# A four-layer encoder trunk on one core: loading and splitting its first input in quarters

## The chip, the cores and the metric

The kernel runs on one core of a Trainium2 chip. The core has TensorE (matrix products and transpositions), VectorE, ScalarE, GpSimd and SyncE (which here issues most DMAs). The metric is the device time of one execution in microseconds (us).

## The reference

Input x is 256 tokens by 1024 columns, float32. Six stages follow each other; each ends in a layer norm of a scaled x plus the stage's result:

```python
def swiglu(x, w_in, w_out):
    gu = x @ w_in
    g, u = gu[..., :D_FF], gu[..., D_FF:]
    return (jax.nn.silu(g) * u) @ w_out

for l in range(2):
    x = layer_norm(ALPHA * x + 0.5 * swiglu(x, ffn_w_in[l, 0], ffn_w_out[l, 0]), ...)
    y = mlstm_mixer(x, ...) if l % 2 == 0 else window_attention(x, ...)
    x = layer_norm(ALPHA * x + y, ...)
    x = layer_norm(ALPHA * x + 0.5 * swiglu(x, ffn_w_in[l, 1], ffn_w_out[l, 1]), ...)
```

`ffn_w_in[l, i]` is 1024 by 5632, `ffn_w_out[l, i]` 2816 by 1024. This document is on the first microseconds of the first `swiglu`.

## The kernel before

**Split numbers.** Every float32 operand of a product is split into a rounded high part and a low part (what is left), and a product is three: high with high, high with low, low with high. ScalarE makes the high part by a cast (`w_hi`, `xT_hi`), VectorE the low part by a subtraction (`w_lo`, `xT_lo`), in each case for weights and for x turned (`xT`).

**Words of weights.** Weights come in words of 128 partitions by 1024 columns (512 KB). A word of `w_in` for the first stage is two blocks of 128 rows by 512 columns, so a word takes 2 blocks x 2 token tiles x 3 = 12 products of 128x512. Class `Weights` loads words from SyncE's queue (`W.load`) into `w_raw` (four buffers), and splits them (`high` and `low`; ten buffers each of `w_hi` and `w_lo`). A buffer of `w_raw` is free for its next word when `low` is done with it. The first word is split in two halves of 512 columns, which ScalarE and VectorE handle one after the other; the load itself is one DMA.

**Turned x.** The products want x with columns on partitions. `to_xT(t, src, bank, halves)` turns token tile t (128 tokens): per half (512 columns) four transpositions on TensorE into one PSUM bank `py`, then `split_evac`, which writes `xT_hi` (ScalarE, or VectorE when `high` is given) and `xT_lo` (VectorE).

**The start.** `load_x(t, h)` loads x in four DMAs of 256 KB (two tiles, two halves), all from ScalarE's queue. `warm(n)` turns the identity n times on TensorE; nothing reads the result. The first stage then runs, in the order of the code: 14 idle turns, the first half of tile 0 turned (VectorE makes both parts), word 0 split, 8 idle turns, and for each of the eight words (m is 0 for g and 1 for u, a is 0 to 3) its 12 products. For words 0 and 1 of m = 0 the order of products is written out in `first_mm`: `mm(t, i, j)` is tile t with x's part i (0 high, 1 low) and the word's part j. Tile 1's first half is turned after the first two products, and both second halves between word 0 and word 1. From word 2 on `b_mm` has no special order.

**What sets the order.** The schedule is the order in which the code emits instructions; each engine works its own list in order. `Paced` keeps a running model of the engines' and queues' times, with which `Weights.fill` decides between products what ScalarE and VectorE split next. So an edit of the start can change the order of later casts and subtractions.

**Waits.** A DMA tells of its landing by one of eight semaphores, which the DMAs of SyncE and ScalarE use in turn; the ninth waits for the landing of the first, and so on.

Of the kernel before, what the change touches and what calls it, by code (L numbers as in the profile page):

```python
# [16 lines left out]
D = 1024  # L17
# [18 lines left out]
FB = [1, 0, 1, 0, 2, 0, 0, 0, 1, 1, 2]  # L36
CT = [0, 1]
DC = 1
EX = [1, 2, 2, 2, 2, 2, 2, 2]
RS = [0, 0, 1, 0, 1, 0, 0, 0, 0, 0, 0, 3, 0, 0, 1, 0, 1, 0, 1, 0, 0, 0, 2, 0, 0, 0, 1, 0, 1, 2, 0, 0, 0, 1, 0, 0, 2, 0, 1, 1, 0, 0, 0, 0, 2, 2, 0, 1]  # L40
XP = [4, 0, 1, 2]
# [24 lines left out]
class Paced:  # L66
# [45 lines left out]
    def load(self, ap, source, engine=None):  # L112
        if engine is not None:
            engine.dma_start(ap, source)
        elif isinstance(source, list):
            for k, src in enumerate(source):
                self.nc.sync.dma_start(ap[:, k].rearrange("p (m f) -> p m f", m=src.shape[1]), src)
        else:
            self.nc.sync.dma_start(ap, source)
        self.moving(0, ap, LANDING, LOADING * int(np.prod(ap.shape[1:])) / 1024, ISSUING)  # L120
# [70 lines left out]
class Weights:  # L191
# [33 lines left out]
    def load(self, most=None):  # L225

        nc = self.nc
        n = 0
        once = False
        while most is None or n < most:  # L230
            next_ = []
            for tag, todo in self.todo.items():
                if not todo:
                    continue
                first = self.first[todo[0]]
                if tag != "w_raw":
                    if self.free[tag] and not once and first < self.used + self.span:
                        next_.append((first, tag, tag))
                elif self.free[tag]:
                    next_.append((first, tag, tag))  # L240
                elif todo[0] < self.send and self.free["v_raw"]:
                    next_.append((first, tag, "v_raw"))
            if not next_:
                break
            _, tag, in_ = min(next_)
            once = once or tag != "w_raw"
            i = self.todo[tag].pop(0)
            pool, bufs = {"w_raw": (self.pool, RAW_BUFS), "v_raw": (self.spool, V_RAW)}.get(in_, (self.rooms, S_RAW))
            t = pool.tile([128, D], F32, name=tag, tag=in_, bufs=bufs)
            nc.load(t.rearrange("p (k f) -> p k f", k=self.words[i]["k"]), self.words[i]["src"])  # L250
            self.raw[i], self.words[i]["in"] = t, in_
            self.free[in_] -= 1
            n += 1
# [72 lines left out]
    def low(self):  # L326

        nc = self.nc
        i, hi = self.half.pop(0)
        p = self.plan[i]  # L330
        k, scale, raw = p["k"], p["scale"], self.raw[p["word"]]
        lo = self.pool.tile([128, D], FR, name="w_lo", tag="w_lo", bufs=RING)
        if i == 0:
            for j in range(2):
                s_ = slice(j * 512, j * 512 + 512)
                nc.vector.tensor_sub(lo[:, s_], raw[:, s_], hi[:, s_].bitcast(F32))
        elif scale is None:
# [109 lines left out]
def trunk_kernel(ctx: ExitStack, tc: tile.TileContext, x, ffn_w_in, ffn_w_out, ln_g, ln_b, ml_w_in, ml_gate_b,  # L447
                 ml_norm_g, ml_w_out, at_w_in, at_sink, at_w_out, out):
    nc = Paced(tc.nc)
# [79 lines left out]
    for j, (kind, l, i, _) in enumerate(stages):  # L529
        if kind == "ffn":  # L530
# [13 lines left out]
            for g in range(SEVENS):  # L544
                c0 = 768 + 512 * g
# [25 lines left out]
    for p in reversed(plan):  # L571
        if p["needs"] is not None:
            q = plan[p["needs"]]
            q["due"] = min(q["due"], p["due"] - p["behind"])

    xt = [state.tile([128, D], F32, name=f"x{t}", tag=f"x{t}") for t in range(2)]

    def load_x(t, h):
        s_ = slice(h * 512, h * 512 + 512)
        nc.load(xt[t][:, s_], x[0, t * 128:(t + 1) * 128, s_], nc.nc.scalar)  # L580

    xT = (state.tile([128, 8, S], FR, name="xT_hi", tag="xT_hi"),
          state.tile([128, 8, S], FR, name="xT_lo", tag="xT_lo"))

    W = Weights(nc, wpool, rooms, words, plan, after)
    load_x(0, 0)
    W.load(1)
    load_x(1, 0)
    W.load(1)
    load_x(0, 1)  # L590
    load_x(1, 1)
    W.load()
    nc.scalar.preload_act_table(AF.Silu)

    ident = consts.tile([128, 128], F32, name="ident")
# [28 lines left out]
    def pair(p, *idx):  # L624
        return p[0][idx], p[1][idx]

    def wbank(shape=(128, 512)):
        return psum.tile(list(shape), F32, name="pw", tag="pw", bufs=4)

    def ybank(shape=(128, 512)):  # L630
        return psum.tile(list(shape), F32, name="py", tag="py", bufs=4)

    A = slice(None)

    def tok(t):
        return slice(t * 128, (t + 1) * 128)

    def split_evac(dst, src, scale=None, high=None, wait=False):
        if scale is None:
            (high or nc.scalar.copy)(dst[0], src)  # L640
            low = lambda: nc.vector.tensor_sub(dst[1], src, dst[0].bitcast(F32))
            if wait:
                W.when_ready(low, dst[0])
            else:
                low()
        else:
            nc.scalar.activation(dst[0], src, AF.Copy, scale=scale)
            nc.vector.scalar_tensor_tensor(dst[1], src, scale, dst[0].bitcast(F32), op0=OP.mult, op1=OP.subtract)

    turned = {}  # L650

    def to_xT(t, src, bank, halves=range(2), high=None):
        for h in halves:
            p = bank((128, 4, 128))
            for k in range(4):
                nc.tensor.transpose(p[:, k], src[:, (4 * h + k) * 128:(4 * h + k + 1) * 128], ident)
            split_evac(pair(xT, A, slice(4 * h, 4 * h + 4), tok(t)), p, high=high)
            turned[t, h] = p

    def warm(n):  # L660

        p = ybank((128, 4, 128))
        for j in range(n):
            nc.tensor.transpose(p[:, j % 4], ident, ident)
# [103 lines left out]
    def emit_x(t, last):  # L768
        if not last:
            to_xT(t, xt[t], ybank)  # L770

    def ffn(l, i, n, pending, last):
        with ExitStack() as ph:
# [9 lines left out]

            start = pending is None
            if start:
                warm(14)
                to_xT(0, xt[0], ybank, (0,), nc.vector.tensor_copy)
                W.split(1)
                warm(8)
            hs, pieces = [], []  # L790

            def tr(hB, t, h):
# [15 lines left out]

            def first_mm(ps, a):

                def mm(t, i, j):
                    for k in (2 * a, 2 * a + 1):
                        nc.tensor.matmul(ps[t], xT[i][:, k, tok(t)], pieces[a][j][:, k % 2], start=i == j == k == 0,
                                         stop=False)

                if a == 1:
                    for t in range(2):
                        to_xT(t, xt[t], ybank, (1,))
                pieces.extend(W.take(1))
                mm(0, 0, 0)  # L820
                if a == 0:
                    to_xT(1, xt[1], ybank, (0,))
                    W.split(2)
                mm(0, 1, 0)
                if a == 0:
                    mm(0, 0, 1)
                mm(1, 0, 0)
                if a == 0:
                    mm(1, 0, 1)
                mm(1, 1, 0)  # L830
                if a == 1:
                    mm(0, 0, 1)
                    mm(1, 0, 1)

# [39 lines left out]
            if start:  # L874
                sg = {}
                for m in range(2):
                    ps = [wbank(), wbank()]
# [132 lines left out]
            ps = [wbank(), wbank()]  # L1010
            pieces = []
# [325 lines left out]
    def attn(l, n, pending, last):  # L1337
        with ExitStack() as ph:
# [98 lines left out]
            def scores(j, between):  # L1437
# [54 lines left out]
            def turn(j, sb, p):  # L1492
# [140 lines left out]
```

## Time and profile before

| | us |
|---|---|
| median of 3 runs | 911.12 (910.35 to 911.18) |
| the profiled execution | 910.79 |
| its span, first to last instruction | 909.1 |
| TensorE busy | 900.3 |
| VectorE busy | 799.6 |
| ScalarE busy | 570.3 |

In the rows of the profile, PE is TensorE's products and transpositions (MATMUL in both cases), PEld its loads of the stationary operand (LDWEIGHTS), DVE is VectorE, ACT is ScalarE, POOL is GpSimd, SP is SyncE; a q behind an engine is its sequencer issuing DMAs. `py<-ident` is an idle turn, `py<-ident,x` a turn of x, `pw<-w_hi,xT_hi` a product. All engine instructions go through one helper, so they share one line (L182) and are told apart by their tiles. A row of the timeline is: start, length, engine, line, operation, tiles, shape, count, and in brackets the engine's idle time before it and what ended it; equal instructions that follow each other are merged. A row of groups ends in: busy us, mean ns of one, idle time before. A row of stretches gives busy us (and count) of PE, PEld, DVE, ACT and POOL, then granted clock, DMA share and GB/s. A DMA issue row ends in its size and the time from issue to landing; a queue row is packets, MB, share of the 16 engines' time.

### The profile page before, as it was taken

The page shows a single profiled execution, that of the slowest core. Times are in us where ns is not written, and L with a number is a line of the kernel's source. Part 1 is how long each engine was busy: PE and PEld are TensorE (multiplying, and loading weights), DVE is VectorE, ACT ScalarE, POOL GpSimd, SP SyncE. Part 2 cuts the span into 40 slices and gives each one's busy share as a digit, 9 for nine tenths or more (in the row PEclk, how much of TensorE's full clock was granted, in tenths as well). Part 3 has the DMA queues.
Part 4 walks back from the last instruction along what each step waited for, and adds up shares of the span by engine and source line. Part 5 has one row for each costly group of instructions (what it writes and reads, how often), then busy time and mean ns, then how long its engine had stood idle before and what let it go on. Part 6 is the DMA issues. An engine that isn't in the chain of part 4 may idle for free.

```text
span 909.1 us, 12461 instructions
## 1 busy us (share of the span) xinstructions
PE 900.3 (99%) x4427; PEld 749.5 (82%) x4427; DVE 799.6 (88%) x961; ACT 570.3 (63%) x785; POOL 152.1 (17%) x190
## 2 busy tenths in 40 slices
PE   9999999999999999999999999999999999999996
PEld 7888888889988888888888888888886788888885
DVE  6999999886799898999988899998868789899986
ACT  5776777356664666776636677765568556676760
POOL 0111123113211011211011112110325301111110
PEclk9999999999999999999999999999999999999999
DMA  8999998546637898998868889986444587899851
GB/s 290 367 330 249 287 276 217 164 138 183 212 106 247 297 237 235 292 278 242 236 197 279 254 248 280 281 220 216 140 140 140 170 294 219 202 296 281 251 140 47
DMA packets 100703, 208.53 MB, mean 229 GB/s; under 512 B 6904, under 2 KB 21264, under 8 KB 100640
## 3 DMA queue, kind: packets, MB, share of 16 engines
q1 hardware_dynamic: 82368, 173.04, 54.4%
q0 software_dynamic: 17696, 33.65, 22.2%
q10 hardware_dynamic: 576, 1.05, 0.3%
q8 instruction: 35, 0.57, 0.2%
q14 instruction: 28, 0.23, 0.1%
HBM read 206.65 MB, written 1.05 MB: 228 GB/s over the span
## 4 chain that ended last, share of the span: by engine, by line
PE 98%; DVE 1%; issue 0%; DVEq 0%; POOL 0%; POOLq 0%
PE pw L182 63%; PE py L182 35%; DVE w_lo L182 0%; DVE x L182 0%; DVE stats L182 0%; DVE e L182 0%; DVE s_raw L182 0%; DVEq L1629 0%; DVE mv L182 0%; POOL ji L597 0%; DVE ident L182 0%; DVE rs L182 0%; DVEq L182 0%; POOLq L597 0%; POOLq L1620 0%
## 5 line engine op out<-in xcount | busy, mean ns | idle before, releaser
L182 DVE TENSOR_TENSOR w_lo<-w_raw,w_hi 128x1024 fp32r<-128x1024 f32 (+1 forms) x213 | 255.8, 1222 | 25.4 <-ACT w_hi L182 23.5
L182 ACT CAST w_hi<-w_raw 128x1024 fp32r<-128x1024 f32 (+1 forms) x213 | 218.9, 1050 | 77.1 <-PE py L182 22.2
L182 DVE TENSOR_TENSOR w_lo<-s_raw,w_hi 128x1024 fp32r<-128x1024 f32 x192 | 228.7, 1220 | 18.8 <-ACT w_hi L182 18.7
L182 ACT CAST w_hi<-s_raw 128x1024 fp32r<-128x1024 f32 x192 | 196.6, 1054 | 58.8 <-PE py L182 25.0
L182 PE MATMUL pw<-w_hi,xT_hi 128*128 128x512 f32 x480 | 189.4, 396 | 0.0
L182 PE MATMUL pw<-w_hi,xT_lo 128*128 128x512 f32 x480 | 186.9, 391 | 0.0
L182 PE MATMUL pw<-w_lo,xT_hi 128*128 128x512 f32 x480 | 186.7, 390 | 0.1
L123 POOL DMA_DIRECT2D s_raw<-in_ffn_w_in_dram x64 | 77.4, 1211 | 484.0 <-DVE s_raw L182 222.3
L182 PE MATMUL py<-w_hi,h_hi 128*128 128x512 f32 x349 | 138.2, 396 | 0.0
L182 PE MATMUL py<-w_hi,h_lo 128*128 128x512 f32 x349 | 136.2, 390 | 0.0
L182 PE MATMUL py<-w_lo,h_hi 128*128 128x512 f32 x349 | 136.0, 390 | 0.0
L182 PEld LDWEIGHTS pw<-w_lo,xT_hi 128*128 128x128 f32 x480 | 90.3, 188 | 18.8 <-DVE w_lo L182 1.3
L182 PEld LDWEIGHTS pw<-w_hi,xT_lo 128*128 128x128 f32 x480 | 90.1, 188 | 19.1
L182 PEld LDWEIGHTS pw<-w_hi,xT_hi 128*128 128x128 f32 x480 | 90.1, 188 | 17.2
L182 PE MATMUL pw<-w_hi,S_lo 128*128 128x512 f32 x256 | 99.7, 389 | 0.0
L182 PE MATMUL pw<-w_lo,S_hi 128*128 128x512 f32 x256 | 99.7, 389 | 0.0
L182 PE MATMUL pw<-w_hi,S_hi 128*128 128x512 f32 x256 | 99.7, 389 | 0.0
L182 DVE TENSOR_TENSOR s_raw<-s_raw,s_raw 128x1024 f32<-128x1024 f32 x64 | 76.8, 1220 | 0.3
L182 PEld LDWEIGHTS py<-w_hi,h_lo 128*128 128x128 f32 x349 | 65.5, 188 | 14.0
L182 PEld LDWEIGHTS py<-w_lo,h_hi 128*128 128x128 f32 x349 | 65.7, 188 | 13.0
L182 PEld LDWEIGHTS py<-w_hi,h_hi 128*128 128x128 f32 x349 | 65.6, 188 | 12.8
L182 PEld LDWEIGHTS pw<-w_lo,S_hi 128*128 128x128 f32 x256 | 48.1, 188 | 10.0
(203 smaller groups left out, 1099.0 us busy)
## 6 DMA issues: line engine op xcount, KB each, us to landing
s_raw<-in_ffn_w_in_dram SPq DMA_DIRECT2D x96, 512.0 KB, 8.0
w_raw<-in_ffn_w_out_dram SPq DMA_DIRECT2D x88, 512.0 KB, 6.2
w_raw<-in_ffn_w_in_dram SPq DMA_DIRECT2D x64, 512.0 KB, 5.6
s_raw<-in_ffn_w_in_dram POOLq DMA_DIRECT2D x64, 512.0 KB, 8.2
w_raw<-in_ml_w_in_dram SPq DMA_DIRECT2D x24, 512.0 KB, 4.4
w_raw<-in_ffn_w_in_dram SPq DMA_DIRECT2D x32, 256.0 KB, 6.1
w_raw<-in_at_w_in_dram SPq DMA_DIRECT2D x12, 512.0 KB, 4.8
w_raw<-in_ml_w_out_dram SPq DMA_DIRECT2D x8, 512.0 KB, 3.8
```

The lines of the kernel that those rows point to most:

```text
L123: self.nc.gpsimd.dma_start(ap, source, accum_op=OP.add)
L182: r = f(out, *args, **kw)
```

## The change

1. x's first 512 columns are loaded in quarters of 256 columns (128 KB). The first quarter of both tiles is issued by ScalarE, the second by SyncE between word 0 and word 1; x's second halves are issued by SyncE after word 1.
2. Word 0 is loaded by two DMAs of one half (256 KB) each.
3. The idle turns are 10 and 3 instead of 14 and 8.
4. x's first halves are turned and split by quarters (`part_xT`), each quarter between products of word 0; the first product needs one quarter of tile 0 and half of word 0.
5. Both second halves are turned late in word 1 instead of ahead of it.

```diff
+WA = 10
+WB = 3
...
-            nc.load(t.rearrange("p (k f) -> p k f", k=self.words[i]["k"]), self.words[i]["src"])
+            to = t.rearrange("p (k f) -> p k f", k=self.words[i]["k"])
+            if i == 0:
+                for k in range(2):
+                    nc.load(to[:, k], self.words[i]["src"][:, k])
+            else:
+                nc.load(to, self.words[i]["src"])
...
-    load_x(0, 0)
+    for t in range(2):
+        load_x(t, 0, 256, nc.nc.scalar)
     W.load(1)
-    load_x(1, 0)
+    for t in range(2):
+        load_x(t, 256, 512)
     W.load(1)
-    load_x(0, 1)
-    load_x(1, 1)
+    for t in range(2):
+        load_x(t, 512, D)
     W.load()
...
+    def part_xT(t, h, q, high=None):
+        if q == 0:
+            turned[t, h] = ybank((128, 4, 128))
+        p = turned[t, h][:, 2 * q:2 * q + 2]
+        c = 4 * h + 2 * q
+        for k in range(2):
+            nc.tensor.transpose(p[:, k], xt[t][:, (c + k) * 128:(c + k + 1) * 128], ident)
+        split_evac(pair(xT, A, slice(c, c + 2), tok(t)), p, high=high)
...
-                warm(14)
-                to_xT(0, xt[0], ybank, (0,), nc.vector.tensor_copy)
+                warm(WA)
+                part_xT(0, 0, 0, nc.vector.tensor_copy)
                 W.split(1)
-                warm(8)
+                warm(WB)
...
+                pieces.extend(W.take(1))
+                mm(0, 0, 0, (0,))
+                if a == 0:
+                    part_xT(1, 0, 0)
+                mm(0, 0, 0, (1,))
+                mm(0, 1, 0)
+                if a == 0:
+                    part_xT(0, 0, 1)
+                    mm(1, 0, 0)
+                    mm(0, 0, 1, (0,))
+                    mm(1, 0, 1, (0,))
+                    part_xT(1, 0, 1)
+                    W.split(2)
+                    mm(1, 1, 0)
+                    mm(0, 0, 1, (1,))
+                    mm(1, 0, 1, (1,))
+                else:
+                    mm(1, 0, 0)
+                    mm(1, 1, 0)
                     for t in range(2):
                         to_xT(t, xt[t], ybank, (1,))
```

What stands in a row on TensorE from the second row of idle turns to word 1's first products (x_72 is tile 0 of x, x_73 tile 1), before:

```order
L182 MATMUL py<-ident 128x128 x8
L182 MATMUL pw<-w_hi,xT_hi 128x512 x2
L182 MATMUL py<-ident,x_73 128x128 x4
L182 MATMUL pw<-w_hi,xT_lo 128x512 x2
L182 MATMUL pw<-w_lo,xT_hi 128x512 x2
L182 MATMUL pw<-w_hi,xT_hi 128x512 x2
L182 MATMUL pw<-w_lo,xT_hi 128x512 x2
L182 MATMUL pw<-w_hi,xT_lo 128x512 x2
L182 MATMUL py<-ident,x_72 128x128 x4
L182 MATMUL py<-ident,x_73 128x128 x4
L182 MATMUL pw<-w_hi,xT_hi 128x512 x2
```

And after, over the same stretch of TensorE's list:

```order
L184 MATMUL py<-ident 128x128 x3
L184 MATMUL pw<-w_hi,xT_hi 128x512
L184 MATMUL py<-ident,x_73 128x128 x2
L184 MATMUL pw<-w_hi,xT_hi 128x512
L184 MATMUL pw<-w_hi,xT_lo 128x512 x2
L184 MATMUL py<-ident,x_72 128x128 x2
L184 MATMUL pw<-w_hi,xT_hi 128x512 x2
L184 MATMUL pw<-w_lo,xT_hi 128x512 x2
L184 MATMUL py<-ident,x_73 128x128 x2
L184 MATMUL pw<-w_hi,xT_lo 128x512 x2
L184 MATMUL pw<-w_lo,xT_hi 128x512 x2
L184 MATMUL pw<-w_hi,xT_hi 128x512 x2
```

The second quarters of both tiles are now turned inside word 0, and the second halves no longer stand between word 0 and word 1 (the last row of each piece is word 1's first).

ScalarE's list from its start to the casts of words 1 to 6, before (`w_hi` of 128x512 is half of word 0, of 128x1024 a whole word):

```order
L114 DMA x_72<-in_x_dram 128x512
L114 DMA x_73<-in_x_dram 128x512
L114 DMA x_72<-in_x_dram 128x512
L114 DMA x_73<-in_x_dram 128x512
L593 ACT_TABLE_LOAD
L182 CAST w_hi<-w_raw 128x512 x2
L182 CAST xT_hi<-py 128x4x128
L182 CAST w_hi<-w_raw 128x1024
L182 CAST xT_hi<-py 128x4x128 x2
L182 CAST w_hi<-w_raw 128x1024 x5
```

And after:

```order
L116 DMA x_72<-in_x_dram 128x256
L116 DMA x_73<-in_x_dram 128x256
L601 ACT_TABLE_LOAD
L184 CAST w_hi<-w_raw 128x512 x2
L184 CAST xT_hi<-py 128x2x128 x3
L184 CAST w_hi<-w_raw 128x1024 x2
L184 CAST xT_hi<-py 128x4x128
L184 CAST w_hi<-w_raw 128x1024
L184 CAST xT_hi<-py 128x4x128
L184 CAST w_hi<-w_raw 128x1024 x3
```

Three casts of quarters of x stand ahead of word 1's cast, where one cast of a half stood; word 2's cast has moved ahead of x's second halves.

VectorE's list over the same stretch, before:

```order
L182 CAST xT_hi<-py 128x4x128
L182 TENSOR_TENSOR xT_lo<-py,xT_hi 128x4x128
L182 TENSOR_TENSOR w_lo<-w_raw,w_hi 128x512 x2
L182 TENSOR_TENSOR xT_lo<-py,xT_hi 128x4x128
L182 TENSOR_TENSOR w_lo<-w_raw,w_hi 128x1024
L182 TENSOR_TENSOR xT_lo<-py,xT_hi 128x4x128 x2
L182 TENSOR_TENSOR w_lo<-w_raw,w_hi 128x1024 x5
```

And after:

```order
L184 CAST xT_hi<-py 128x2x128
L184 TENSOR_TENSOR xT_lo<-py,xT_hi 128x2x128
L184 TENSOR_TENSOR w_lo<-w_raw,w_hi 128x512 x2
L184 TENSOR_TENSOR xT_lo<-py,xT_hi 128x2x128 x3
L184 TENSOR_TENSOR w_lo<-w_raw,w_hi 128x1024 x2
L184 TENSOR_TENSOR xT_lo<-py,xT_hi 128x4x128 x2
L184 TENSOR_TENSOR w_lo<-w_raw,w_hi 128x1024 x4
```

Here too word 2's `w_lo` has moved ahead of the low parts of x's second halves.

More of the change, by code (lines that the diff above doesn't have):

```diff
@@ L576, in trunk_kernel, with load_x @@
     xt = [state.tile([128, D], F32, name=f"x{t}", tag=f"x{t}") for t in range(2)]
-    def load_x(t, h):
-        s_ = slice(h * 512, h * 512 + 512)
-        nc.load(xt[t][:, s_], x[0, t * 128:(t + 1) * 128, s_], nc.nc.scalar)
+    def load_x(t, c0, c1, engine=None):
+        nc.load(xt[t][:, c0:c1], x[0, t * 128:(t + 1) * 128, c0:c1], engine)
     xT = (state.tile([128, 8, S], FR, name="xT_hi", tag="xT_hi"),
@@ L809, in first_mm, with mm @@
             def first_mm(ps, a):
[L811 to L816, printed above, removed]
+                def mm(t, i, j, ks=range(2)):
+                    for k in ks:
+                        nc.tensor.matmul(ps[t], xT[i][:, 2 * a + k, tok(t)], pieces[a][j][:, k],
+                                         start=i == j == k == a == 0, stop=False)
+                pieces.extend(W.take(1))
[17 more added lines that the diff above has]
+                    mm(1, 1, 0)
                     for t in range(2):
                         to_xT(t, xt[t], ybank, (1,))
[L819 to L831, printed above, removed]
                     mm(0, 0, 1)
```

## The prediction

> **What bounds the kernel now.** I read the page's busy shares and its chain first, then the tensor engine's waits and stretches, then the first 15 us engine by engine, then the DMA issues and bytes of the same stretch.
>
> ```profile
> PE 900.3 (99%) x4427; PEld 749.5 (82%) x4427; DVE 799.6 (88%) x961; ACT 570.3 (63%) x785; POOL 152.1 (17%) x190
> ...
> PE 98%; DVE 1%; issue 0%; DVEq 0%; POOL 0%; POOLq 0%
> ...
> PEld pw L182 <- DVE w_lo L182: 0.4, 1, 0.4
> ...
> 14.50:560.00 545.50, 545.50 (x2639) 458.51 (x2639) 490.77 (x564) 350.92 (x457) 85.09 (x85) 1.00 0.82 244
> ```
>
> TensorE is the whole chain (98%). The third row is the list of waits of its weight loads between 16 and 560 us: one wait, 0.4 us. So whatever the start loses or saves before about 14.5 us is carried to the end one for one, and nothing there can be hidden. The change edits exactly this start. Its weight loads (start, length) are:
>
> ```profile
> 1.71 2.85 PEld L182 LDWEIGHTS py<-ident 128*128 128x128 f32 x14 [1.71 <-DVE ident L182]
> 4.55 0.85 PEld L182 LDWEIGHTS py<-ident,x 128*128 128x128 f32 x4
> 5.39 1.28 PEld L182 LDWEIGHTS py<-ident 128*128 128x128 f32 x8
> 6.65 0.30 PEld L182 LDWEIGHTS pw<-w_hi,xT_hi 128*128 128x128 f32 x2
> 6.99 0.59 PEld L182 LDWEIGHTS py<-ident,x 128*128 128x128 f32 x4
> 8.52 0.19 PEld L182 LDWEIGHTS pw<-w_lo,xT_hi 128*128 128x128 f32 x1 [0.41 <-DVE w_lo L182]
> 10.01 1.03 PEld L182 LDWEIGHTS py<-ident,x 128*128 128x128 f32 x8
> 12.74 0.88 PEld L182 LDWEIGHTS pw<-w_lo,xT_hi 128*128 128x128 f32 x4
> 13.66 0.19 PEld L182 LDWEIGHTS pw<-w_hi,xT_hi 128*128 128x128 f32 x1
> 14.21 0.19 PEld L182 LDWEIGHTS pw<-w_lo,xT_hi 128*128 128x128 f32 x1 [0.36 <-DVE w_lo L182]
> ```
>
> The 14 idle turns, 4 turns of x and 8 more idle turns fill 1.71 to 6.65; the first product starts at 6.65; words 0 and 1 (24 products) and the other 12 turns of x end at 13.66, where word 2 begins, and a late w_lo there costs about 0.2 (load 14.21 instead of 13.89, of which 0.1 is hidden by loading ahead). The mark to compare is therefore 13.9: word 2 running without stalls.
>
> One thing is not in the busy shares: turns are slower at first.
>
> ```profile
> L182 PEld LDWEIGHTS py<-ident 128*128 128x128 f32 x18 | 3.7, 225 | 1.7 <-DVE ident L182 1.7
> ...
> L182 PEld LDWEIGHTS py<-ident 128*128 128x128 f32 x4 | 0.5, 141 | 0.0
> ...
> 2.00:6.15 4.15, 4.15 (x21) 4.15 (x20) 0.30 (x1) 1.96 (x3) 0.00 (x0) 1.00 0.91 310
> ```
>
> The first row covers 1.7 to 6.1 us, the second 6.3 to 14 us: the same instruction, 225 ns against 141. Turns follow each other at 0.21 early (4 in 5.39-4.55) and at about 0.125 later (8 in 11.01-10.01, including a gap). The array ran slow until about 6.2, that is 4.5 us after its first turn, though the granted clock of 2.00 to 6.15 stands as 1.00 in the third row (third number from its end). The speed changed inside a row of idle turns, before any product. I assume that products are slowed by the same factor, 0.43 instead of 0.23 (0.92 for the 4 from 12.74 to 13.66); before, no product ran that early, so the price is bounded by 0.23 and 0.46.
>
> **The change, part by part.**
>
> *Fewer idle turns (14 to 10, 8 to 3).* Ten turns at 0.20 (2.85/14) end at 3.74, against 4.55. If x's first quarter is there, its two turns end at 4.18. Landing:
>
> ```profile
> x<-in_x_dram ACTq DMA_DIRECT2D x1, 256.0 KB, 3.7
> w_raw<-in_ffn_w_in_dram SPq DMA_DIRECT2D x1, 512.0 KB, 4.7
> ...
> w_raw<-in_ffn_w_in_dram SPq DMA_DIRECT2D x1, 512.0 KB, 7.2
> ...
> q1 hardware_dynamic: 153, 0.31, 25.1%
> q10 hardware_dynamic: 144, 0.26, 18.6%
> ...
> q1 hardware_dynamic: 271, 0.52, 32.0%
> ...
> q1 hardware_dynamic: 477, 0.94, 39.0%
> q10 hardware_dynamic: 360, 0.67, 28.0%
> ...
> q1 hardware_dynamic: 824, 1.60, 46.3%
> q10 hardware_dynamic: 576, 1.05, 30.8%
> ```
>
> The first two rows are the first issues (both at 0.79): x's half lands at 4.5, word 0 at 5.5. The third is word 1, issued at 1.29 and landed at 8.5. The pairs are MB moved by SP's queue (q1) and ScalarE's (q10) by 4.2, 7.0 and 9.7 us: 0.57, 1.61 and 2.65 together; the single row is SP's by 5.0. Half of x's first 256 KB cannot land later than 4.5; by bytes it lands near 3.5. I take "there by 3.74"; if not, up to 0.7 is lost.
>
> *Halves of word 0.* By order of issue 0.52 MB (two quarters of x, half a word) stand ahead of its first half, which the first pair reaches near 4.1; landings lag the bytes by about 0.4 (word 0's 0.52 MB are through by 5.0, it lands at 5.5). So 4.5 for the first half, 5.2 for the second (0.79 MB), x's second quarters by 5.8, word 1 (1.57 MB) at 7.3, the rest of x at 8.6, word 2 (2.62 MB) at 10.1.
>
> ```profile
> 5.48 1.14 ACT L182 CAST w_hi<-w_raw 128x512 fp32r<-128x512 f32 x2 [1.16 <-DMA w_raw<-in_ffn_w_in_dram]
> 7.86 0.59 ACT L182 CAST xT_hi<-py 128x512 fp32r<-128x512 f32 x1 [1.24 <-PE py L182]
> 8.54 1.05 ACT L182 CAST w_hi<-w_raw 128x1024 fp32r<-128x1024 f32 x1
> ...
> 42.47 0.65 ACT L182 ACTIVATE sg<-pw 128x256 f32<-128x256 f32 x2
> ...
> 5.85 0.69 DVE L182 CAST xT_hi<-py 128x512 fp32r<-128x512 f32 x1 [4.19 <-PE py L182]
> ...
> L182 DVE TENSOR_TENSOR x<-x,pw 128x256 f32<-128x256 f32 x2 | 0.8, 412 | 0.0
> ```
>
> The cast of half a word takes 0.57 (1.14/2): 4.5 to 5.1. On VectorE the quarter's cast starts 0.45 after the last turn's load (5.40 to 5.85 before) and takes 0.41 instead of 0.69: 4.63 to 5.04, and 0.11 later (6.54 to 6.65 before) the first product can start: 5.15. That is 1.5 earlier than 6.65.
>
> *What gives it back: the slow array.* From 5.15 to 6.2 the sequence is product (0.43), two turns (0.42), half a product: some 0.45 lost. The second half's cast (5.2 to 5.75) is in time.
>
> *What gives it back: order.* The three products and turns that follow run at full pace: 6 products and two pairs of turns bring the last quarter's turns to end at 8.1 (6.25 + 6 x 0.23 + 2 x 0.25). Its cast stands on ScalarE ahead of word 1's, which was free to go at word 1's landing before (8.54). Now: 0.28 after the turns (7.58 to 7.86 before) the cast starts, 8.4; 0.33 later (0.65/2) word 1's starts, 8.75; 1.05 later it is done, and the product at 9.85. Word 0's last 4 products end at 9.03 (8.1 + 4 x 0.23). So 0.8 us of new wait, on ScalarE's word 1, though word 1 landed at 7.3.
>
> *The rest of the start.* 8 products (1.84), 8 turns (1.0) and 4 products (0.88) bring word 2 to 13.57. x's second halves (8.6, wanted 11.7) and word 2 (cast 10.1 to 11.2, w_lo by 12.4) have 2 us to spare each. The w_lo wait at 14.21 goes, since w_lo of word 2 now stands on VectorE ahead of the late xT_lo; what is late next is x's last xT_lo and word 3's w_lo, by my count just in time, bounds 0 to 0.2.
>
> *SP's queue.* It gets five issues more.
>
> ```profile
> 0.79 0.97 SPq L119 DMA_DIRECT2D w_raw<-in_ffn_w_in_dram  x2
> ...
> 0.79 2.21 ACTq L114 DMA_DIRECT2D x<-in_x_dram  x4
> 3.03 1.28 ACT L593 ACT_TABLE_LOAD   x1 [3.03 <-issue]
> ```
>
> One takes about 0.5 (0.97/2), so word 2 is issued near 4.5 instead of 1.8 (it is the eighth on SP, the third before) and waits for word 0's first half by its semaphore. By then over 1.5 MB stand ahead of it, so the queue never runs dry: nothing, and if it did, the 2 us of slack above cover it. ScalarE loses two issues, so its table load (ended at 4.3) ends about 1 earlier; the first cast wants it at 4.5, so nothing. By a rule of the Trainium skill (DMA: Bandwidth & Descriptors, "Issuing engines are not separate DMA queues") moving x's issues from one engine to another would only save the issuer's time; then all of the gain is from splitting and order, which is how I count it, and no term changes.
>
> *Later order.* A few casts and sums between 25 and 60 us change places.
>
> ```profile
> 12.93 4.73 DVE L182 TENSOR_TENSOR w_lo<-w_raw,w_hi 128x1024 fp32r<-128x1024 f32 x4
> ...
> 18.94 1.23 DVE L182 TENSOR_TENSOR w_lo<-w_raw,w_hi 128x1024 fp32r<-128x1024 f32 x1 [1.27 <-ACT w_hi L182]
> ...
> 23.00:60.00 37.00, 37.00 (x171) 30.76 (x170) 36.63 (x39) 26.36 (x33) 4.99 (x4) 1.00 1.06 348
> ```
>
> VectorE is full there (36.63 of 37), but its w_lo are ready 2 to 4 us ahead of use: words 2 to 5 are the first row, word 6's, the second, is done at 20.2 and wanted near 25 (13.9 + 4 words of 12 products, 2.73 each). I cost it at 0; without that cover it is one DVE piece, 1.2, so the bounds are 0 to 1.2.
>
> Sum: mark 13.9 becomes 13.6: -0.3 of the profiled execution's 910.79 (span 909.1 and 1.7 around it), 910.5. The median of the three runs, 911.12, is 0.3 above that execution; from it the forecast is 910.8. Measurement here can tell about 0.2%, 1.8 us, from no change.
>
> **The rivals.**
>
> *A: the slow array lasts longer (slower).* TensorE is now idle for about 0.35 between its last idle turn (4.8) and the first product, and the idle turns were what ran while the array sped up. If the 4.5 us count begins anew at 5.15, it is slow until 9.65. Then 8 products and 6 turns, up to the last quarter's turns, take 4.6 instead of 2.95, word 1's product goes from 9.85 to 11.5, and the end from -0.3 to +1.35: 912.4. It makes the kernel slower at all if the speed-up falls after about 6.8 (0.3 at half pace), by 0.2% only after about 12 (another 0.5, paid by word 1's own products from 11.5). For it: the idle hole. Against it: 90% of 1.71 to 6.2 is still busy. The Trainium skill (TensorE: Matmul & The Clock Gate, Part 1) has the array at half clock until a window of about 3.4 us has been busy, with windows that run free of the kernel's start; by that rule the same happens a window later, at about 9.6 (an estimate from its figure: 6.2 + 3.4), and at another moment in each run. That page of the Trainium skill, in its Part 4 on transposes, says that turns do not count as activity; the rows of 225 and 141 ns above, both of turns, speak against that.
>
> *B: word 0's half lands no sooner (no change).* The two queues share the engines: by 4.2 they had moved 0.26 and 0.31 MB, neither kept to an order. If the second quarter and both halves move together, the first half lands with the second, near 5.4, the first product starts at 6.1, all behind it shifts by 0.65: +0.35, 911.4.
>
> *C: the word 1 cast is no limit and the array is fast at 5.15 (faster).* 24 products (5.5) and 14 turns (1.75) from 5.15 end at 12.4: -1.5, 909.6. That is the floor, and still within 0.2%. Half of it, with the speed-up somewhat earlier, is 910.0.
>
> *D: a new stall by the changed order after 25 us.* One piece late: +0.9, more with several.
>
> **How the numbers follow.** Forecast 0.55; A 0.18; B 0.11; C 0.11; D 0.05. Forecast's own range 910.3 to 911.2 (clock 0.3, landing 0.2, last xT_lo 0.2). The range, 909.8 to 912.4, reaches into C and to A. Faster by over 0.2% needs more than C's floor: 0.03. Slower by over 0.2% needs A beyond 12 or D with several stalls: 0.05. Within: 0.92.
>
> **What would show it.** Right: first `pw` weight load near 5.15, 225 ns turns until about 6.2, ScalarE's word 1 cast near 8.75 directly behind a 128x256 xT_hi cast, a wait of TensorE for w_hi of about 0.8 there, word 2 near 13.6, and no new wait up to 560. Wrong: a first product after 5.8 (B), products of 0.4 spacing after 6.5 (A), no wait at word 1 (C), weight-load waits between 25 and 75 (D).

## The result, and the profile after

The changed kernel takes 912.76 us (median of 19 runs, 910.91 to 914.17), the kernel before on the same chip 910.9 (19 runs, 909.94 to 911.74): ratio 1.0021, 95% interval 1.0015 to 1.0027. The change makes the kernel slower by 1.86 us. The prediction said 910.8 with a range of 909.8 to 912.4: wrong in its sign and just outside its range. The profiled execution is 912.67, its span 911.0.

TensorE's weight loads of the first 17 us, after (start, length, tiles, count, idle time before):

```profile
1.71 1.99 PEld L184 LDWEIGHTS py<-ident 128*128 128x128 f32 x10 [1.71 <-DVE ident L184]
4.79 0.29 PEld L184 LDWEIGHTS py<-ident,x 128*128 128x128 f32 x2 [1.08 <-DMA x<-in_x_dram]
5.06 0.66 PEld L184 LDWEIGHTS py<-ident 128*128 128x128 f32 x3
6.06 0.29 PEld L184 LDWEIGHTS pw<-w_hi,xT_hi 128*128 128x128 f32 x1 [0.34 <-issue]
...
7.08 0.76 PEld L184 LDWEIGHTS pw<-w_hi,xT_lo 128*128 128x128 f32 x2
...
10.49 0.17 PEld L184 LDWEIGHTS py<-ident,x 128*128 128x128 f32 x1 [0.20 <-issue]
10.63 0.30 PEld L184 LDWEIGHTS pw<-w_hi,xT_lo 128*128 128x128 f32 x2
10.97 0.42 PEld L184 LDWEIGHTS pw<-w_lo,xT_hi 128*128 128x128 f32 x2
12.31 0.30 PEld L184 LDWEIGHTS pw<-w_hi,xT_hi 128*128 128x128 f32 x2 [0.91 <-ACT w_hi L184]
...
15.82 0.19 PEld L184 LDWEIGHTS pw<-w_hi,xT_hi 128*128 128x128 f32 x1
16.06 0.19 PEld L184 LDWEIGHTS pw<-w_lo,xT_hi 128*128 128x128 f32 x1
```

Read from the top: the ten idle turns are over at 3.71, and TensorE waits 1.08 for x (idle stretches like this one are called holes below). A second hole of 0.34 stands ahead of the first product, at 6.06 instead of 6.65. Two loads of `xT_lo` take 0.76 at 7.08, two of `w_lo` 0.42 at 10.97: the array runs slow until 10.54 (before: 6.15), where the trace has a record of the array's clock going to full speed (called the speed-up below). Then TensorE waits 0.91 for word 1, and word 2 starts at 15.82 instead of 13.66. The mark (word 2 without stalls, which before was its start and 0.2 for the late `w_lo`) goes from 13.9 to 15.82, +1.92; the profiled executions differ by 1.88. All of it is lost in the first 16 us: word 2's third weight load moves from 14.32 to 16.29, by 1.97, and the load that stands at 560.10 before stands at 562.08 after, 1.98 later. The list of waits of TensorE's weight loads between 16 and 560 us has one row, as before:

```profile
PEld pw L184 <- DVE w_lo L184: 0.4, 1, 0.4
```

ScalarE in the same stretch, and then the first DMA issues (both at 0.79; KB, us to landing):

```profile
4.60 0.62 ACT L184 CAST w_hi<-w_raw 128x512 fp32r<-128x512 f32 x1 [1.60 <-DMA w_raw<-in_ffn_w_in_dram]
...
10.94 0.37 ACT L184 CAST xT_hi<-py 128x256 fp32r<-128x256 f32 x1 [1.54 <-PE py L184]
11.21 2.00 ACT L184 CAST w_hi<-w_raw 128x1024 fp32r<-128x1024 f32 x2
```

```profile
w_raw<-in_ffn_w_in_dram SPq DMA_DIRECT2D x1, 256.0 KB, 3.8
x<-in_x_dram ACTq DMA_DIRECT2D x1, 128.0 KB, 4.0
```

Word 0's first half lands at 4.58, x's first quarter at 4.75: 0.24 later than the half of x, twice its size, landed before. Word 1's cast (11.21) stands right behind the last quarter's `xT_hi`, as forecast.

### The profile page after: what moved, and what is told of

The parts are those of the page before. It is cut to its first block, busy times and chain, and to the rows that moved or that the text cites. A ratio compares the mean times of both kernels' runs of the same rounds, so it can differ in the third digit from the quotient of the medians.

```text
span 911.0 us, 12453 instructions
## 1 busy us (share of the span) xinstructions
PE 900.8 (99%) x4418; PEld 748.8 (82%) x4418; DVE 799.7 (88%) x963; ACT 571.2 (63%) x787; POOL 151.7 (17%) x190
## 4 chain that ended last, share of the span: by engine, by line
PE 98%; DVE 1%; DMA 0%; ACT 0%; issue 0%; DVEq 0%
PE pw L184 63%; PE py L184 35%; DMA x<-in_x_dram 0%; DVE x L184 0%; DVE stats L184 0%; ACT w_hi L184 0%; DVEq L1651 0%; ACT xT_hi L184 0%; DVE mv L184 0%; DVE rs L184 0%
## 5 line engine op out<-in xcount | busy, mean ns | idle before, releaser
L184 PEld LDWEIGHTS pw<-w_hi,S_hi 128*128 128x128 f32 x256 | 48.1, 188 | 10.1
```

Source lines behind the costliest of these rows:

```text
L184: r = f(out, *args, **kw)
```

## The experiments

Theory when they began: the quarter lands late, the holes that this leaves in TensorE's work put off its speed-up, and the real products that were to use the time run slow; word 1's late cast is a second, separate loss. Rivals: only one of these counts, or a moved order does.

All runs in one table (us; "speed-up" is the clock record in the profiled execution, "wait" that for word 1's `w_hi`, "word 2" its first weight load; these four columns are each from one execution, the median is of all runs; ratio to the kernel before on the same chip, whose median there was 910.85 to 910.95):

| kernel | first product | speed-up | wait | word 2 | median | ratio, 95% |
|---|---|---|---|---|---|---|
| before | 6.65 | 6.15 | none | 13.66 | 910.9 | |
| after | 6.06 | 10.54 | 0.91 | 15.82 | 912.76 | 1.0021 (1.0015 to 1.0027) |
| fill_15_5 | 6.25 | 6.49 | 0.92 | 14.10 | 911.61 | 1.0009 (1.0000 to 1.0018) |
| before_10_8 | 7.29 | 7.85 | none | 14.31 | 911.10 | 1.0004 (0.9995 to 1.0012) |
| x_halves | 6.08 | 9.33 | none | 14.52 | 912.23 | 1.0015 (1.0005 to 1.0024) |
| word1_first | 6.03 | 9.65 | none | 14.65 | 913.90 | 1.0037 (1.0023 to 1.0051) |
| halves_fill | 6.47 | 7.69 | none | 14.01 | 910.76 | 1.0002 (0.9994 to 1.0011) |
| x_on_sp | 5.95 | 11.15 | 0.89 | 16.17 | 913.55 | 1.0027 (1.0013 to 1.0040) |
| x0_sp_x1_act | 5.70 | 7.53 | 0.92 | 14.26 | 911.81 | 1.0011 (1.0001 to 1.0020) |
| x_sp_half | 6.04 | 6.89 | none | 13.42 | 911.06 | 1.0002 (0.9993 to 1.0011) |
| word0_whole | 6.22 | 11.37 | none | 15.52 | 912.56 | 1.0019 (1.0009 to 1.0029) |
| before_word0_halves | 7.11 | 6.71 | none | 14.01 | 911.86 | 1.0011 (1.0002 to 1.0020) |
| after_again, one run | 6.05 | 11.11 | 0.86 | 16.03 | 913.72 | |
| before_again, one run | 6.64 | 5.65 | none | 13.63 | 911.09 | |

### Do the holes make the loss?

**fill_15_5**: the changed kernel with its holes filled.

```diff
-WA = 10
-WB = 3
+WA = 15
+WB = 5
```

> The changed kernel with 15 and 5 idle turns instead of 10 and 3; loads and order as changed. Theory 1 (the holes in TensorE's row of idle turns, 1.1 us before x's first turns and 0.3 before the first product, are why the array stayed slow until 10.5): without holes the turns speed up near 6.2 as before the change, the first product stays near 6.1, word 2 starts near 13.9 instead of 15.8, and the time is 910.8. Rival (the slow time has nothing to do with the holes; it ends late by chance or because products started early): turns and products stay slow until about 10.5, and the time is 912.8 to 913.2.

Its weight loads:

```profile
6.25 0.31 PEld L184 LDWEIGHTS pw<-w_hi,xT_hi 128*128 128x128 f32 x1
...
10.57 0.30 PEld L184 LDWEIGHTS pw<-w_hi,xT_hi 128*128 128x128 f32 x2 [0.92 <-ACT w_hi L184]
```

The first product comes 0.19 later than in the changed kernel, the speed-up 4 us sooner, and the kernel is 1.15 us faster (912.76 to 911.61). Seven turns that compute nothing win that. The wait for word 1 stays as it was (0.92).

**before_10_8**: the kernel before with a hole.

```diff
-                warm(14)
+                warm(10)
```

> The kernel before the change with 10 idle turns ahead of x's first turns instead of 14, nothing else. Theory 1: TensorE is idle from 3.8 to 4.5, x's turns start at 4.5 as before, but the array stays slow until 9.5 to 10.5 and the time is 912.0 to 912.5, 1.2 or more slower than before. Rival: idle turns only fill time, all starts as before, 910.9.

```profile
4.89 0.71 PEld L182 LDWEIGHTS py<-ident,x 128*128 128x128 f32 x4 [1.18 <-DMA x<-in_x_dram]
5.59 1.72 PEld L182 LDWEIGHTS py<-ident 128*128 128x128 f32 x8
7.29 0.55 PEld L182 LDWEIGHTS pw<-w_hi,xT_hi 128*128 128x128 f32 x2
```

The hole is there (1.18) and the speed-up comes at 7.85, not at 9.5 or later, and the time hardly moves (911.10): the expected 912.0 and more was a miss. The reason is in the second row: eight idle turns stand behind the hole, and they, not products, run slow (0.21 each), until 7.3; word 2 is only 0.65 later. Half of that may not be the hole's at all, since x, loaded as before, landed 0.33 later in this execution (4.84 against 4.51):

```profile
x<-in_x_dram ACTq DMA_DIRECT2D x1, 256.0 KB, 4.1
```

The reading that fits both runs is that a hole costs what the real work in the slow time costs: the changed kernel has 3 idle turns behind its hole and then products.

**after_again** and **before_again**: both kernels unchanged, one more profile each.

> The changed kernel once more, for one more profile. Theory (the speed-up comes at the end of the first busy window of about 3.4 us, and the windows lie at another place in each execution): the spacing of turns and products halves at another moment than 10.5, somewhere between 8 and 11.5, while the landings stay within 0.1. Rival (a count that starts with the first product or the end of the hole): again 10.4 to 10.6.

> The kernel before once more, for one more profile. Theory (windows of about 3.4 us at another place in each execution; TensorE busy from 1.71 on): the spacing of turns halves anywhere between 5 and 7.9, not necessarily at 6.15 again, landings within 0.1, and the first product stays near 6.65 as long as it is before word 0's cast. Rival (a fixed count of 4.5 us from the first turn): 6.1 to 6.2 again.

Weight loads of the changed kernel's second profile, at the places where the first had 0.30 and 0.42, and of the kernel before's, where the first had 1.28:

```profile
10.69 0.51 PEld L184 LDWEIGHTS pw<-w_hi,xT_lo 128*128 128x128 f32 x2
11.24 0.41 PEld L184 LDWEIGHTS pw<-w_lo,xT_hi 128*128 128x128 f32 x2
```

```profile
5.39 1.04 PEld L182 LDWEIGHTS py<-ident 128*128 128x128 f32 x8
6.64 0.30 PEld L182 LDWEIGHTS pw<-w_hi,xT_hi 128*128 128x128 f32 x2 [0.21 <-ACT w_hi L182]
```

The same kernel with x landing at the same time (4.74 and 4.75) speeds up at 11.11 in place of 10.54, the kernel before at 5.65 in place of 6.15. So no fixed count from the first turn or from the hole does it. Before, the difference costs nothing: the first product stands at 6.64, and a wait of 0.21 for word 0 takes what the faster turns give. In the changed kernel products bear it.

What fits all the profiles is a grid of stretches of about 3.4 us whose place differs from execution to execution, at whose end the array becomes fast if TensorE was busy enough in it. Below are such stretches counted back from the speed-up (start and end, length, PE busy): the changed kernel's last two, before_10_8's last, and the last but one of x_on_sp, word0_whole and x_halves.

```profile
3.71:7.12 3.41, 2.73 (x11) 1.81 (x10) 1.57 (x4) 1.24 (x2) 0.00 (x0) 1.00 1.04 374
7.12:10.54 3.42, 3.42 (x11) 2.53 (x11) 1.33 (x3) 0.75 (x2) 0.00 (x0) 1.00 1.03 374
```

```profile
4.43:7.85 3.42, 2.96 (x13) 2.95 (x14) 1.77 (x3) 1.14 (x2) 0.00 (x0) 1.00 1.01 374
```

```profile
4.32:7.73 3.41, 3.06 (x12) 2.14 (x11) 2.28 (x5) 1.61 (x3) 0.00 (x0) 1.00 0.89 284
```

```profile
4.54:7.95 3.41, 3.05 (x10) 2.38 (x11) 2.21 (x5) 1.51 (x3) 0.00 (x0) 1.00 1.06 385
```

```profile
2.50:5.91 3.41, 2.71 (x13) 2.14 (x11) 0.37 (x1) 1.29 (x3) 0.00 (x0) 1.00 0.94 347
```

In all 14 profiles, stretches at whose end the array stayed slow were busy for 2.71 to 3.06 of 3.41 (and less, where they began before the first turn); those that ended in full speed for 2.96 to 3.42. The two overlap between 2.96 and 3.06: ends of PE's work are modelled, so how busy is enough stays open, near nine tenths by this measure. The Trainium skill (TensorE: Matmul & The Clock Gate, Part 1) describes such windows of about 3.4 us that run free of the kernel's start; the two pairs of profiles agree. The granted clock in these rows is 1.00 while the array is slow, and does not show it.

The traces hold one more sign of the grid: the record of full speed lasts 901.12, 897.71 or 894.29 us in all 14 of them and nothing in between, that is, it ends a whole number of steps of 3.41 after it began. The grid also says what a hole can be blamed for. With TensorE busy without a hole from 1.71 on, the first full stretch ends between 5.12 and 8.53, wherever the grid lies (an estimate: 1.71 and one or two steps). The changed kernel's 10.54 and 11.11 lie outside that, so its holes did put the speed-up off; before_10_8's 7.85 lies inside, so that profile does not show that its hole did.

### Word 1's late cast

**x_halves**: x's first halves as two transfers of 256 KB from ScalarE.

```diff
     for t in range(2):
-        load_x(t, 0, 256, nc.nc.scalar)
+        load_x(t, 0, 512, nc.nc.scalar)
     W.load(1)
-    for t in range(2):
-        load_x(t, 256, 512)
     W.load(1)
```

> The changed kernel, but x's first 512 columns come as two DMAs of 256 KB (2 KB rows) from ScalarE, as before the change, instead of four of 128 KB (1 KB rows); the turns stay in quarters. Theory 2 (the two queues take turns row by row, so rows of 1 KB get half the share of word 0's 2 KB rows): 256 KB of x land no later than the 128 KB did (4.75), near 4.5, and word 0's first half lands later than 4.58. Rival (a landing goes by bytes and order of issue): x's 256 KB land at 5.3 or later. Time: 912.3 to 912.8 by theory 2 (the hole is still there, a little shorter), 913.3 by the rival.

Its first issue of x, ScalarE's word 1 cast, and TensorE at word 1:

```profile
x<-in_x_dram ACTq DMA_DIRECT2D x1, 256.0 KB, 4.0
```

```profile
9.31 1.05 ACT L184 CAST w_hi<-w_raw 128x1024 fp32r<-128x1024 f32 x1
10.40 0.37 ACT L184 CAST xT_hi<-py 128x256 fp32r<-128x256 f32 x1
```

```profile
10.90 0.41 PEld L184 LDWEIGHTS pw<-w_hi,xT_hi 128*128 128x128 f32 x2
```

Twice the bytes land at the same moment (4.77, against 4.75). That word 0's half would suffer was a miss: it landed at 4.54. Word 1, now SyncE's third issue and not its fifth, lands at 7.34 instead of 8.69, and the planner (`Paced` with `Weights.fill`), which goes by its own model of the landings, puts word 1's cast ahead of the last quarter's: no wait. The median gains 0.5 us, though the two intervals overlap; the holes remain.

**word1_first**: the changed kernel with that cast moved by hand.

```diff
                     mm(1, 0, 1, (0,))
+                    W.split(2)
                     part_xT(1, 0, 1)
-                    W.split(2)
```

> The changed kernel with word 1 split ahead of the last quarter of x instead of behind it. Theory 3 (TensorE's wait of 0.9 at 12.3 for word 1's w_hi is there only because its cast stands behind the last quarter's): the cast runs at 9.4 to 10.5, the wait goes, word 2 starts near 15.0 instead of 15.8, 911.9. Rival (the wait moves to xT_lo of tile 1, which now stands behind word 1's w_lo): 912.5 to 912.8.

Its weight loads at word 2, and VectorE:

```profile
14.65 0.19 PEld L184 LDWEIGHTS pw<-w_hi,xT_hi 128*128 128x128 f32 x1
16.80 0.19 PEld L184 LDWEIGHTS pw<-w_lo,xT_hi 128*128 128x128 f32 x1 [1.97 <-DVE w_lo L184]
```

```profile
14.33 1.29 DVE L184 TENSOR_TENSOR xT_lo<-py,xT_hi 128x512 fp32r<-128x512 f32 x2 [2.43 <-ACT xT_hi L184]
15.54 2.35 DVE L184 TENSOR_TENSOR w_lo<-w_raw,w_hi 128x1024 fp32r<-128x1024 f32 x2
```

The wait at word 1 goes, and one of 1.97 comes at word 2: the planner, which starts from the new order, puts both `xT_lo` of x's second halves ahead of word 2's `w_lo`, and these wait 2.43 for their casts with word 2 behind them. At 913.90 it is slower than the changed kernel; neither expectation had this wait. The order here is not free to edit one line at a time.

**halves_fill**: x_halves and fill_15_5 together.

```diff
-WA = 10
-WB = 3
+WA = 15
+WB = 5
...
-        load_x(t, 0, 256, nc.nc.scalar)
+        load_x(t, 0, 512, nc.nc.scalar)
...
-    for t in range(2):
-        load_x(t, 256, 512)
```

> x's first 512 columns as two 256 KB transfers from ScalarE (as in x_halves) together with 15 and 5 idle turns (as in fill_15_5). Theory (two separate losses: holes of TensorE that put off the speed-up, and word 1 landing and cast late): both go; spacing halves near 6.5, first product near 6.3, no wait at word 1, word 2 near 13.5, time 910.2 to 910.8. Rival (one cause only, the holes; x_halves and fill_15_5 gain the same thing in two ways): as fill_15_5, 911.4 to 911.8, word 2 at 14.0 or later.

Both losses go, the hole of 1.08 (0.36 is left of it) and the wait, and the time is that of the kernel before: 912.76 to 910.76. Taken one at a time the two edits gained 1.15 and 0.53, together 2.00. That there are two losses is shown by the rows: fill_15_5 keeps its wait of 0.92 without a hole, and here there is none. How much the second is worth is not: halves_fill is 0.85 ahead of fill_15_5, but their intervals overlap, and in the two profiles word 2 is only 0.09 ahead (14.01, which is the rival's mark of 14.0 or later), because x, loaded as in x_halves, landed at 5.09 in this execution and not at 4.77, and the speed-up came at 7.69.

### Why the quarter is late

The packets and MB that SyncE's queue (q1) and ScalarE's (q10) had moved by 2.6 us, first before, then after:

```profile
q10 hardware_dynamic: 57, 0.12, 14.6%
q1 hardware_dynamic: 8, 0.02, 3.4%
```

```profile
q1 hardware_dynamic: 40, 0.08, 37.7%
q10 hardware_dynamic: 11, 0.01, 1.2%
```

And after, from 3.4 to 3.8 alone:

```profile
q1 hardware_dynamic: 53, 0.10, 67.1%
q10 hardware_dynamic: 53, 0.05, 35.8%
```

Two things stand here. ScalarE's queue was ahead at first before, and is behind after. And while both run, they move about equal numbers of packets, one row of a tile each (in the steps of 0.4 from 2.6 to 3.8: 10 and 9, 23 and 27, 53 and 53): a row of x's quarter is 1 KB, one of a word 2 KB, so x gets half the bytes. By 4.2, ScalarE's queue had moved 144 packets before (the prediction's row) and 145 after. The Trainium skill (DMA: Bandwidth & Descriptors, Queues, rings and completion order) has an engine take its queues in turn, a packet of several descriptors at a time; the 53 and 53 agree with equal turns, and how many rows one turn takes no row here shows.

**word0_whole** and **before_word0_halves**: the halving of word 0 taken out of the changed kernel, and put alone into the kernel before (the same lines, the other way).

```diff
-            if i == 0:
-                for k in range(2):
-                    nc.load(to[:, k], self.words[i]["src"][:, k])
-            else:
-                nc.load(to, self.words[i]["src"])
+            nc.load(to, self.words[i]["src"])
```

> The changed kernel with word 0 loaded by one DMA of 512 KB, as before. Theory (a 512 KB transfer on SyncE starts to move later than one of 256 KB, so that ScalarE's queue had 57 packets against 8 by 2.6 us before, and 11 against 40 after the halving; the quarter was late for that): ScalarE's queue is ahead again by 2.6 us (40 packets or more against 15 or fewer), the quarter lands at 3.6 to 4.2, the hole ahead of x's turns is at most 0.5, word 0 lands at about 5.4. Rival (rows of 1 KB are what makes the quarter late): quarter at 4.6 or later, the hole of 1.0 stays.

> The kernel before with word 0 alone loaded by two DMAs of 256 KB. Theory (the halving puts word 0's first half ahead of x): word 0's first half at about 4.6, x's half of 2 KB rows at 4.7 to 4.9 instead of 4.5, a hole of 0.2 to 0.4 ahead of x's turns, the first product between 6.3 and 7.0, time within 0.5 of the kernel before. Rival (the halving leaves x alone): x at 4.5, no hole, the first product as before or earlier.

Queues by 2.6 us, first word0_whole, then before_word0_halves, and then their issues of x:

```profile
q10 hardware_dynamic: 44, 0.05, 8.7%
q1 hardware_dynamic: 6, 0.01, 6.9%
```

```profile
q1 hardware_dynamic: 30, 0.06, 14.4%
q10 hardware_dynamic: 12, 0.02, 3.3%
```

```profile
x<-in_x_dram ACTq DMA_DIRECT2D x1, 128.0 KB, 3.7
```

```profile
x<-in_x_dram ACTq DMA_DIRECT2D x1, 256.0 KB, 4.2
```

The lead changes hands with word 0's size, in both directions: beside a SyncE transfer of 512 KB ScalarE's queue starts first, beside one of 256 KB it starts second. The other traces agree: by 2.6 us ScalarE's queue had moved 44 to 57 packets against 5 to 8 in the four with word 0 whole, and 7 to 12 against 28 to 40 in the seven where its first half goes first. With the lead lost, x landed 0.24 later in the changed kernel (4.75 against 4.51) and 0.52 in the kernel before (5.03 against 4.51). How much of that is the lead's is open, since landings of the very same loads differ by up to 0.33 between executions (4.51 and 4.84, before and before_10_8; 4.77 and 5.09, x_halves and halves_fill). The other half of the theory missed: without the halving the quarter lands at 4.51, not by 4.2. It is exactly where 256 KB landed before, with as many packets. So beside a word, halving the row of x won nothing in these runs.

In time, word0_whole gains nothing measurable on the changed kernel (912.56), though the planner's order leaves no wait for word 1 in it: word 0 is now what is late (5.53), a hole of 0.74 stands ahead of the first product, and the speed-up comes at 11.37. before_word0_halves is 0.9 us slower than the kernel before, more than the 0.5 expected, with a hole of 0.51 and the first product at 7.11: this part of the change loses by itself.

**x_on_sp**: all first quarters on SyncE, ahead of word 0, with WB at 5.

```diff
-WB = 3
+WB = 5
...
-        load_x(t, 0, 256, nc.nc.scalar)
+        load_x(t, 0, 256)
```

> The changed kernel with all of x's first quarters issued by SyncE ahead of word 0 instead of by ScalarE (10 and 5 idle turns). Theory (the two queues share the DMA engines row by row, so ScalarE's 1 KB rows got half the share of the 2 KB rows of words; ahead of the words in one queue they do not share): the quarter lands at 3.3 to 3.7 instead of 4.75, no hole of TensorE before x's turns, word 0's half at about 4.5, first product near 5.3, turns' spacing halves by about 6.5, word 2 near 13.5, time 910.2 to 910.8. Rival (the quarter's landing is a fixed latency or the price of short rows, whatever queue carries it): quarter at 4.4 or later, the hole of about 1 us stays, spacing halves after 8, time 912 or more.

```profile
x<-in_x_dram SPq DMA_DIRECT2D x1, 128.0 KB, 2.6
```

```profile
5.95 0.29 PEld L184 LDWEIGHTS pw<-w_hi,xT_hi 128*128 128x128 f32 x1 [0.75 <-ACT w_hi L184]
```

With no other queue beside it, and first in its own, the quarter lands at 3.41 (1.34 sooner), and the first hole is gone: neither a fixed latency nor the short row made it late. But word 0's half now lands at 5.25 instead of 4.58, a hole of 0.75 stands one step further on, the speed-up comes at 11.15, and the time is 913.55. The part of the theory that spoke of the time was a miss.

**x0_sp_x1_act** and **x_sp_half**: tile 0 on SyncE ahead of word 0, tile 1 on ScalarE (one 256 KB transfer); first a quarter (10 and 5 idle turns), then a half and more turns. Their lines, one after the other (both take out the same lines of x):

```diff
+WB = 5
...
-    for t in range(2):
-        load_x(t, 0, 256, nc.nc.scalar)
+    load_x(0, 0, 256)
+    load_x(1, 0, 512, nc.nc.scalar)
     W.load(1)
-    for t in range(2):
-        load_x(t, 256, 512)
+    load_x(0, 256, 512)
     W.load(1)
```

```diff
+WA = 13
+WB = 6
...
+    load_x(0, 0, 512)
+    load_x(1, 0, 512, nc.nc.scalar)
     W.load(1)
     W.load(1)
```

> Tile 0's first quarter on SyncE ahead of word 0, tile 1's first half as one 256 KB transfer from ScalarE, tile 0's second quarter on SyncE behind word 0 (10 and 5 idle turns). Row-share theory: quarter at about 3.5, tile 1's half (2 KB rows, equal share) by 4.8, first product near 5.3, word 2 near 13.5, time 910.2 to 910.9. Rival (whatever lands first is late because two queues are open at once): quarter at 4.3 or later, first product 5.8 or later, time 911.5 or more.

> Tile 0's first 512 columns as one 256 KB transfer on SyncE ahead of word 0, tile 1's on ScalarE, 13 and 6 idle turns: what the runs so far point to (x's landing without a hole, the turns as cover, word 1's cast ahead of the third quarter's). Theory (the losses are holes that put off the speed-up, and word 1's late cast): x at about 4.2, word 0's first half at about 5.2, first product at 5.9 to 6.1, no hole over 0.3, spacing halves before 7.8, no wait at word 1, word 2 at 13.0 to 13.4, time 909.9 to 910.5, at or below the kernel before. Rival (x ahead in SyncE's queue only moves the hole to word 0, as in x_on_sp): a hole of 0.5 or more ahead of the first product, spacing halves after 9, time 911.5 or more.

In x0_sp_x1_act the quarter lands at 3.76, and tile 1's half, from ScalarE, at 3.93:

```profile
x<-in_x_dram SPq DMA_DIRECT2D x1, 128.0 KB, 3.0
x<-in_x_dram ACTq DMA_DIRECT2D x1, 256.0 KB, 3.1
```

So two open queues alone do not make x late. Word 0's half lands at 5.01, which leaves a hole of 0.50; the speed-up comes at 7.53, and the wait for word 1 (0.92) is back. The theory is nearer for the quarter, the rival for the time (911.81). But that time is not the price of this start: word 2's third load is only 0.39 behind the kernel before's (14.71), the load of 560.10 is 1.41 behind (561.51). Between the two stand 1.9 us of waits of weight loads for VectorE and ScalarE, where the kernels before and after have one of 0.4. That points to a moved order of later work, rival D of the prediction, which the change itself did not meet. x_sp_half has no hole and no wait:

```profile
6.04 0.33 PEld L184 LDWEIGHTS pw<-w_hi,xT_hi 128*128 128x128 f32 x1
...
13.42 0.19 PEld L184 LDWEIGHTS pw<-w_hi,xT_hi 128*128 128x128 f32 x1
```

Its word 2 is 0.24 ahead of the kernel before's, the third load, behind the late `w_lo`, 0.45 (13.87 against 14.32); at 560 us 0.23 of that is left. Its median (911.06 against 910.92) is not ahead, and the expected 909.9 to 910.5 was a miss: a gain of that size is below what these runs can tell. No version here beats the kernel before.

## Why the prediction was wrong, point by point

- **"I take 'there by 3.74'": failed.** The quarter landed at 4.75, later than the bound that the step itself gave ("cannot land later than 4.5"). Bytes were divided where packets count: with word 0 whole, as before, the quarter still landed at 4.51 (word0_whole). And the step held x's queue as it was while the change altered what ran beside it; that is the other 0.24, by these two profiles. The first product was at 6.06, not 5.15: 0.91 lost, where the step allowed up to 0.7.
- **"The array ran slow until about 6.2 ... some 0.45 lost": failed.** It ran slow until 10.54. The hole that was to come ahead of the first product was seen and priced at nothing in the forecast. From the first product to the end of the last quarter's turns it took 4.60 (6.06 to 10.66), where the forecast had 2.95 and rival A exactly 4.6: 1.65 lost. A had the right cause (the hole) and the right price (products 0.43 apart), and a chance of 0.18; it fell on top of the late quarter, which the range did not add. Its count of 4.5 us from the first product also seems to fit (4.48), but the second profile (5.06) shows that as chance.
- **The wait of 0.8 for word 1: right** (0.91), at the place and behind the cast that were named. It was charged to the change in full, and x_halves and halves_fill show that an order without it exists.
- **The rest of the start: right.** From word 1's product to word 2: 3.51, forecast 3.72. The late `w_lo` at word 2 is gone, as said. Together 0.91 + 1.65 - 0.10 (cast and turns around word 1) - 0.21 = 2.25, by which word 2 (15.82) is behind the forecast's 13.57.
- **Word 0's first half at 4.5: right in the number** (4.58), **by luck in the reason**: both first quarters of x were to be through ahead of it, and they landed after it, at 4.75 and 5.73. Rival B's cause is out, though its sign, a first product after 5.8, came true through x. **Word 1 at 7.3: wrong** (8.69), without a price, since its cast waited for its turn on ScalarE until 11.21.
- **Later order at nothing: right**; rival D is out by the single wait of 0.4.
- **"No term changes" by the rule on issuing engines: misapplied.** The Trainium skill (DMA: Bandwidth & Descriptors, Issuing engines are not separate DMA queues) has all these DMAs run on the same 16 engines and interleave. The sums by 4.2 us are not far apart, 0.50 MB after and 0.56 in x_on_sp; but that only the issuer's time is at stake does not hold here, where the quarter's landing moved by 1.34 us with the queue and the place in it.

What stays open: how busy a stretch must be; why SyncE's first transfer starts sooner as a half word than as a whole one, and how much of x's landing that sets; and whether the wider spread of the changed kernel's runs (3.3 us, against 1.8) is the speed-up's moving place, since only profiled runs show that place.

## What to carry to other kernels

Idle turns at a kernel's start are cover twice over: they bring the array to full speed, and they are what runs slow until then. Whoever cuts them to start real work sooner should ask whether TensorE stays busy without a hole until the speed-up, and price the first products at half pace until a stretch of 3.4 us has been full. And a transfer is not made early by making it small: look at which queue starts first and at what runs beside it, in packets, and at how far the same load's landing differs between executions (0.33 here).

## What the runs showed of the hardware

The array's speed-up came between 5.65 and 6.15 us in the same kernel, and at 10.54 and 11.11 in the other: a moment that differs by half a microsecond with x's landing within 0.03. Full speed then lasted a whole number of steps of 3.41 us in all 14 traces. Two queues of DMAs shared the engines by packets (53 and 53) and not by bytes (0.10 and 0.05 MB). SyncE's queue had the lead over ScalarE's first quarter of x when its own first transfer was 256 KB (40 to 11 packets by 2.6 us), and not when it was 512 KB (6 to 44).
